# Gated layers of a two-layer transformer: nine of eleven feature pairs as a 2 by 2 block product with seven products

## The chip, the core and the metric

One core of a Trainium2 chip runs the whole program. The metric is the device time of one execution in microseconds (us); lower is better. All times are from the hardware profile or from timed executions.

## What is computed

The reference runs one sequence of 512 tokens with 1024 features, in float32, through a conformer convolution layer, a gated layer, a dilated attention layer, a second gated layer, and then a retention block with its own feed-forward part. The change touches the two gated layers only:

```python
def swiglu(h, w_gate, w_up, w_down):
    return (jax.nn.silu(h @ w_gate) * (h @ w_up)) @ w_down

    h = rmsnorm(x, norm_ffn[i])
    x = x + swiglu(h, ffn_w_gate[i], ffn_w_up[i], ffn_w_down[i])
```

`w_gate` and `w_up` are 1024 x 2816 each, `w_down` is 2816 x 1024. The 2816 hidden features are 22 tiles of 128, or eleven pairs of tiles.

## The kernel before

Features lie on the 128 partitions and the 512 tokens along the free dimension. `xT` is the residual stream (8 tiles of 128 x 512), `R` the reciprocal root of the mean square, broadcast over the partitions.

Every float32 product is made from three reduced-precision products (`mm3`): an operand is split into a rounded high part and the low part that is left, and high x high, high x low and low x high are added in one PSUM bank. For an activation the parts are `xh`, `xl`; for a weight `whi`, `wlo`. Weights come from HBM in blocks of 128 x 1024 elements (`raw`, four buffers). `Stream` loads them in the order of `weight_plan`, and `split_to` makes `whi` on ScalarE (line 127 in the profile's rows is its rounding copy) and `wlo` on VectorE. `get` hands the next block to the matmuls and first splits up to four blocks counted from the one that it hands out; there are four buffers of `whi` and of `wlo`, so the split of a block waits until TensorE has finished with the block four places earlier. Line 80 is the helper `Meter`, through which all VectorE, GpSimd and TensorE instructions are recorded.

Each engine runs its instructions in the order in which the program issues them; that order is written out by hand. `half_tick` is called after every two contraction tiles, and `after(n, fn)` puts a piece of work n ticks later.

A gated layer (`ffn`) takes a pair of feature tiles at a time. `group` multiplies the pair's gate columns with the 8 tiles of the input (2 x 8 x 3 matmuls of 512 tokens), a second `group` the up columns. Then, for each tile, VectorE multiplies both results by `R`, ScalarE applies Silu, VectorE multiplies the two, ScalarE makes the high part `hh` and VectorE the low part `hl` (lines 986 and 990 are the two ScalarE steps). The input's own split for these products is made before the root is known; `R` is applied to the results. `norm_root` gets `R` some 2.5 ticks into the layer. When all 22 tiles are there, four groups over 22 contraction tiles form the down product.

Of the kernel before, what the change touches and what calls it, by code (L numbers as in the profile page):

```python
# [13 lines left out]
S = 512  # L14
# [3 lines left out]
KF = 22  # L18
# [36 lines left out]
POOLW = (0, 0, 0, 0)  # L55
LN1 = (3, 5, 2, 5)
BACK = 2.5
WAIT = 1
ROOT = 0.5
HD_SCALE = 64 ** -0.5  # L60
# [24 lines left out]
class Stream:  # L85


    def __init__(self, nc, V, G, raw_p, w_p, specs, n_raw, n_split):
        self.nc, self.V, self.G = nc, V, G
        self.raw_p, self.w_p, self.specs = raw_p, w_p, specs  # L90
        self.n_raw, self.n_split = n_raw, n_split
        self.raw, self.hl = {}, {}
        self.limit = 1 << 30
        self.on_pool = ()
        self.wait = 0
        self.i_load = self.i_split = self.i_use = 0

    def shape(self, i):
        _, _, nk, cols = self.specs[i]
        return nk, sum(n for _, n in cols)  # L100

    def load_to(self, n):
        while self.i_load < min(n, len(self.specs)):
            w, k0, nk, cols = self.specs[self.i_load]
            nk, nc_ = self.shape(self.i_load)
            t = self.raw_p.tile([128, 1024], F32, tag="raw", name="raw")
            v = t[:, 0:nk * nc_].rearrange("p (k c) -> p k c", k=nk)
            o = 0
            for c0, n_ in cols:
                self.nc.sync.dma_start(  # L110
                    out=v[:, :, o:o + n_],
                    in_=w[k0 * 128:(k0 + nk) * 128, c0:c0 + n_].rearrange("(k p) c -> p k c", p=128),
                )
                o += n_
            self.raw[self.i_load] = t
            self.i_load += 1

    def split_to(self, n):
        while self.i_split < min(n, len(self.specs), self.limit):
            i = self.i_split  # L120
            nk, nc_ = self.shape(i)
            self.load_to(i + 1)
            raw = self.raw.pop(i)[:, 0:nk * nc_]
            h = self.w_p.tile([128, 1024], F32R, tag="whi", name="whi")
            l = self.w_p.tile([128, 1024], F32R, tag="wlo", name="wlo")
            hv, lv = h[:, 0:nk * nc_], l[:, 0:nk * nc_]
            self.nc.scalar.activation(out=hv, in_=raw, func=AF.Copy)  # L127
            E = self.G if i in self.on_pool else self.V
            E.tensor_tensor(out=lv, in0=raw, in1=hv.bitcast(F32), op=ALU.subtract)
            self.hl[i] = (  # L130
                hv.rearrange("p (k c) -> p k c", k=nk),
                lv.rearrange("p (k c) -> p k c", k=nk),
            )
            self.i_split += 1
            self.load_to(self.i_split + self.n_raw - self.wait)

    def get(self):
        i = self.i_use
# [5 lines left out]
def weight_plan(A):  # L144
    specs = []

    def cols(w, c0, n, kt, step=4):
        for k in range(0, kt, step):
            specs.append((w, k, min(step, kt - k), [(c0, n)]))

    for j in range(KD):
        for k, n in ((0, 4), (4, 4)) if j else ((0, 2), (2, 2), (4, 4)):
            specs.append((A["conv_w_pw1"][0], k, n, [(128 * j, 128), (D + 128 * j, 128)]))
    def pair(w, ca, cb, ks=((0, 4), (4, 4))):
        for k, n in ks:
            for c in (ca, cb):
                specs.append((w, k, n, [(c, 256)]))

    pair(A["conv_w_pw2"][0], 0, 256)
    for j in (2, 3):  # L160
        cols(A["conv_w_pw2"][0], 256 * j, 256, KD)

    def ffn(l):
        for j in range(KF // 2):
            cols(A["ffn_w_gate"][l], 256 * j, 256, KD)
            cols(A["ffn_w_up"][l], 256 * j, 256, KD)
        for j in range(4):
# [121 lines left out]
def body(nc, tc, A, out):  # L289
# [3 lines left out]
    with ctx:  # L293
# [284 lines left out]
        with tc.tile_pool(name="c1", bufs=1) as c1, tc.tile_pool(name="c1s", bufs=1, side="right") as c1s:  # L578
# [90 lines left out]
            def add(j, t):  # L669
                V.tensor_tensor(out=cc[j], in0=cc[j], in1=t, op=ALU.add)  # L670
# [302 lines left out]

        def ffn(l, gname, goff):
            with tc.tile_pool(name=f"ff{l}", bufs=1) as fp:
                hh = [fp.tile([128, S], F32R, name=f"hh{k}") for k in range(KF)]
                hl = [fp.tile([128, S], F32R, name=f"hl{k}") for k in range(KF)]
                after(2, norm_root)
                for jj in range(KF // 2):
                    pg = group(KD, *xop)  # L980
                    pu = group(KD, *xop)
                    for m in range(2):
                        j = 2 * jj + m
                        a = tmp.tile([128, S], F32, tag="t1", name="a")
                        V.tensor_tensor(out=a, in0=pg[m], in1=R, op=ALU.mult)
                        ACT.activation(out=a, in_=a, func=AF.Silu)  # L986
                        b = tmp.tile([128, S], F32, tag="t2", name="b")
                        V.tensor_tensor(out=b, in0=pu[m], in1=R, op=ALU.mult)
                        V.tensor_tensor(out=b, in0=a, in1=b, op=ALU.mult)
                        ACT.activation(out=hh[j], in_=b, func=AF.Copy)  # L990
                        V.tensor_tensor(out=hl[j], in0=b, in1=hh[j].bitcast(F32), op=ALU.subtract)
                for j in range(0, KD, 2):
                    resid(group(KF, lambda k: hh[k], lambda k: hl[k]), j, gname, goff)

        ffn(0, "norm_mix", 8)

# [671 lines left out]
```

## Time and profile before

| | |
|---|---|
| median of 3 timed runs | 1663.43 us (1660.7 to 1664.26) |
| the profiled execution | 1660.89 us, its span 1659.1 us |
| granted TensorE clock, mean | 0.995 |
| TensorE busy | 98% of the span, 7972 matmuls |
| VectorE busy | 52%, 1254 instructions |
| ScalarE busy | 35%, 871 instructions |

The span runs from the first to the last instruction. Matmuls are pipelined, so the length that a row gives for one matmul is longer than the distance to the next; the rate is read from starts. For VectorE and ScalarE too the next instruction may begin a little before the recorded end of the last.

### The profile page before, as it was taken

What the parts mean: (1) busy time and instruction counts of PE and PEld (TensorE: products, weight loads), DVE (VectorE), ACT (ScalarE), POOL (GpSimd) and SP (SyncE); (2) the same over time, 40 slices, a digit from 0 to 9 for tenths busy, and PEclk for the clock granted to TensorE, in tenths of its full rate; (3) what the DMA queues carried; (4) which work ended last, traced back from release to release, by engine and by line L of the source; (5) the groups of instructions that cost most, each with busy time, mean ns of one, the idle gap of its engine ahead of it and who ended that gap; (6) DMA issues with size and microseconds to landing.
All of it is one profiled execution on the core that took longest, in us unless ns stands there. A gap on an engine that the chain in (4) does not pass through costs nothing.

```text
span 1659.1 us, 19926 instructions
## 1 busy us (share of the span) xinstructions
PE 1629.4 (98%) x7972; PEld 1366.3 (82%) x7972; DVE 869.2 (52%) x1254; ACT 586.0 (35%) x871; POOL 181.3 (11%) x151
## 2 busy tenths in 40 slices
PE   9998999999999999999999999999999999999997
PEld 6787888888888878888888888888888888888886
DVE  7996644444423345664444434346776545544226
ACT  5623532332322234343323223234543543333210
POOL 4786100000000000000000000000323200000000
PEclk9999999999999999999999999999999999999999
DMA  7331323232232432132323332342232323233321
GB/s 205 116 123 45 102 90 102 89 100 89 85 108 91 128 102 74 52 115 89 98 89 94 102 96 92 105 130 73 64 102 64 127 65 114 89 102 102 102 89 51
DMA packets 157221, 159.85 MB, mean 96 GB/s; under 512 B 6490, under 2 KB 148937, under 8 KB 157129
## 3 DMA queue, kind: packets, MB, share of 16 engines
q1 hardware_dynamic: 157128, 158.59, 30.9%
q8 instruction: 62, 1.02, 0.2%
q14 instruction: 31, 0.25, 0.0%
HBM read 154.56 MB, written 5.57 MB: 97 GB/s over the span
## 4 chain that ended last, share of the span: by engine, by line
PE 85%; DVE 8%; ACT 3%; issue 2%; DMA 1%; POOL 1%; SPq 0%; DVEq 0%; ACTq 0%; POOLq 0%
PE mm L80 73%; PE dn L80 6%; PE pv L80 2%; DMA raw<-in_conv_w_pw 1%; DVE cb L80 1%; DVE cc L80 1%; DVE ca L80 1%; DVE wlo L80 1%; PE o L80 1%; ACT whi L127 1%; DVE y L80 1%; PE po L80 1%; DVE rp L80 0%; DVE sdl L80 0%; PE tl L80 0%
## 5 line engine op out<-in xcount | busy, mean ns | idle before, releaser
L80 DVE TENSOR_TENSOR wlo<-raw,whi 128x1024 fp32r<-128x1024 f32 (+1 forms) x278 | 336.0, 1222 | 519.2 <-ACT whi L127 519.1
L80 PE MATMUL mm<-xh,whi 128*128 128x512 f32 (+1 forms) x1472 | 570.6, 388 | 1.9 <-ACT whi L127 1.5
L80 PE MATMUL mm<-xl,whi 128*128 128x512 f32 (+1 forms) x1472 | 568.2, 386 | 1.6 <-DVE xl L80 1.2
L80 PE MATMUL mm<-xh,wlo 128*128 128x512 f32 (+1 forms) x1472 | 567.8, 386 | 0.4 <-DVE wlo L80 0.4
L127 ACT ACTIVATE whi<-raw 128x1024 fp32r<-128x1024 f32 (+1 forms) x282 | 285.9, 1031 | 522.2 <-PE mm L80 316.8
L80 PEld LDWEIGHTS mm<-xl,whi 128*128 128x128 f32 x1472 | 277.4, 188 | 58.2 <-DVE xl L80 4.1
L80 PEld LDWEIGHTS mm<-xh,whi 128*128 128x128 f32 x1472 | 277.5, 189 | 58.1 <-issue 1.8
L80 PEld LDWEIGHTS mm<-xh,wlo 128*128 128x128 f32 x1472 | 277.3, 188 | 56.7 <-DVE wlo L80 1.4
L80 PE MATMUL mm<-hh,whi 128*128 128x512 f32 x352 | 136.9, 389 | 0.0
L80 PE MATMUL mm<-hl,whi 128*128 128x512 f32 x352 | 136.9, 389 | 0.0
L80 PE MATMUL mm<-hh,wlo 128*128 128x512 f32 x352 | 136.9, 389 | 0.0
L80 POOL TENSOR_TENSOR r<-v,mhalf 128x4 f32<-128x4 f32 x9 | 12.9, 1429 | 986.1 <-DVE v L80 986.1
L80 PEld LDWEIGHTS mm<-hl,whi 128*128 128x128 f32 x352 | 66.1, 188 | 13.8
L80 PEld LDWEIGHTS mm<-hh,wlo 128*128 128x128 f32 x352 | 66.1, 188 | 13.8
L80 PEld LDWEIGHTS mm<-hh,whi 128*128 128x128 f32 x352 | 66.1, 188 | 13.6
L80 PE MATMUL dn<-wlo,gh 128*128 128x512 f32 x176 | 68.6, 390 | 0.1
L80 PE MATMUL dn<-whi,gh 128*128 128x512 f32 x176 | 68.5, 389 | 0.0
L80 PE MATMUL dn<-whi,gl 128*128 128x512 f32 x176 | 68.5, 389 | 0.0
L990 ACT ACTIVATE hh<-b 128x512 fp32r<-128x512 f32 x44 | 27.8, 632 | 78.9 <-DVE b L80 78.9
L80 DVE TENSOR_TENSOR b<-mm,R 128x512 f32<-128x512 f32 x44 | 30.2, 686 | 44.5 <-PE mm L80 44.5
L986 ACT ACTIVATE a<-a 128x512 f32<-128x512 f32 x44 | 27.8, 632 | 72.7 <-DVE a L80 72.7
L80 DVE TENSOR_TENSOR hl<-b,hh 128x512 fp32r<-128x512 f32 x44 | 30.5, 692 | 30.8 <-ACT hh L990 30.8
(257 smaller groups left out, 1780.3 us busy)
## 6 DMA issues: line engine op xcount, KB each, us to landing
raw<-in_ffn_w_gate SPq DMA_DIRECT2D x44, 512.0 KB
raw<-in_ffn_w_up SPq DMA_DIRECT2D x44, 512.0 KB
raw<-in_w_up SPq DMA_DIRECT2D x44, 512.0 KB
raw<-in_ffn_w_down SPq DMA_DIRECT2D x40, 512.0 KB
raw<-in_w_down SPq DMA_DIRECT2D x22, 512.0 KB
raw<-in_w_in SPq DMA_DIRECT2D x20, 512.0 KB
raw<-in_attn_w_qkv SPq DMA_DIRECT2D x18, 512.0 KB
raw<-in_conv_w_pw SPq DMA_DIRECT2D x30, 256.0 KB
```

The costliest lines, as they stand in the source:

```text
L80: return fn(*args, **kw)
L127: self.nc.scalar.activation(out=hv, in_=raw, func=AF.Copy)
L986: ACT.activation(out=a, in_=a, func=AF.Silu)
L990: ACT.activation(out=hh[j], in_=b, func=AF.Copy)
```

## The change

In each gated layer the first two pairs (`NPL = 2`) stay as they were. In the other nine, the pair's gate and up columns together are treated as a 2 by 2 block matrix (two feature tiles by two halves of the contraction), and the input as a 2 by 2 block matrix (two halves of the contraction by two halves of the tokens). The block product is made with seven block products in place of eight. A block of weights is 4 contraction tiles x 128 gate and 128 up columns. One of the seven ("role" 0 to 6) is 24 matmuls of 256 columns into one bank: gate in its first half, up in its second.

On the weight side four loaded blocks (`a11`, `a21`, `a22`, `a12`) give seven operands, with four additions on VectorE (`source`), each of which is then split. `a12` gets a buffer of its own, and loads are issued when the buffer's last use has been split (`free`). On the input side, the blocks are normalized once `R` is known (`normed`), four differences and sums are formed, and seven operands split (`hi`, `lo`); these 26 steps are dealt out three at a time over the first two pairs. An unused tile of 192 bytes a partition (`PADB`) stands ahead of these operands' tiles and moves them. After the products, VectorE combines the seven outputs into four blocks; Silu and the multiply work on 256 tokens and are issued one and two roles later. The high and low parts of hidden features are no longer made in each pair but during the last pair and during the down product, up to three tiles ahead of use (`LOOK`). The program also reserves 128 in place of 1024 bytes for descriptors of GpSimd transfers.

```diff
+NPL = 2
+LOOK = 3
+PADB = 192
...
+        self.loads, self.need = [], []
+        free = {"raw": [], "a12": []}
+        for i, (w, k0, nk, cols) in enumerate(specs):
+            if not isinstance(w, tuple):
+                new = [((i,), [(w, k0, nk, cols)], "raw", i)]
+            elif k0 == 0:
+                new = [((i, n), [(m, k, 4, [(cols + c, 128)]) for m in w], tag, i + e) for n, k, c, tag, e in (
+                    ("a11", 0, 0, "raw", 2), ("a21", 0, 128, "raw", 4), ("a22", 4, 128, "raw", 6), ("a12", 4, 0, "a12", 5))]
+            else:
+                new = []
+            for name, parts, tag, e in new:
+                self.loads.append((name, parts, tag, free[tag], len(free[tag])))
+                free[tag].append(e)
+            n = len(self.loads)
+            self.need.append(n - (3, 1, 1)[k0] if isinstance(w, tuple) and k0 < 3 else n)
...
+    def free(self):
+        if self.i_load == len(self.loads):
+            return False
+        _, _, tag, ends, n = self.loads[self.i_load]
+        n -= self.n_raw - self.wait if tag == "raw" else 1
+        return n < 0 or ends[n] < self.i_split
+    def source(self, i):
+        w, role, _, _ = self.specs[i]
+        if not isinstance(w, tuple):
+            return self.raw.pop((i,))
+        r = {n: self.raw[i - role, n] for n in ("a11", "a21", "a22", "a12") if (i - role, n) in self.raw}
+        add = lambda out, a, b: self.V.tensor_tensor(out=out, in0=a, in1=b, op=ALU.add)
+        if role == 1:
+            self.s = self.sum_p.tile([128, 1024], F32, tag="s1", name="s1", bufs=1)
+            add(self.s, r["a21"], r["a22"])
+        elif role == 2:
+            add(self.s, r["a11"], self.s)
+            add(r["a21"], r["a11"], r["a21"])
+        elif role == 5:
+            add(self.s, r["a12"], self.s)
+        return (r["a11"], self.s, self.s, r.get("a12"), r["a21"], self.s, r["a22"])[role] if role else r["a11"]
 
     def split_to(self, n):
         while self.i_split < min(n, len(self.specs), self.limit):
             i = self.i_split
-            nk, nc_ = self.shape(i)
-            self.load_to(i + 1)
-            raw = self.raw.pop(i)[:, 0:nk * nc_]
+            w, _, nk, _ = self.specs[i]
+            self.load_to(self.need[i])
+            raw = self.source(i)
+            n_ = raw.shape[1]
             h = self.w_p.tile([128, 1024], F32R, tag="whi", name="whi")
             l = self.w_p.tile([128, 1024], F32R, tag="wlo", name="wlo")
-            hv, lv = h[:, 0:nk * nc_], l[:, 0:nk * nc_]
+            hv, lv = h[:, 0:n_], l[:, 0:n_]
             self.nc.scalar.activation(out=hv, in_=raw, func=AF.Copy)
             E = self.G if i in self.on_pool else self.V
             E.tensor_tensor(out=lv, in0=raw, in1=hv.bitcast(F32), op=ALU.subtract)
...
             self.i_split += 1
-            self.load_to(self.i_split + self.n_raw - self.wait)
+            while self.free():
+                self.load_to(self.i_load + 1)
...
-        for j in range(KF // 2):
+        for j in range(NPL):
             cols(A["ffn_w_gate"][l], 256 * j, 256, KD)
             cols(A["ffn_w_up"][l], 256 * j, 256, KD)
+        for j in range(NPL, KF // 2):
+            for role in range(7):
+                specs.append(((A["ffn_w_gate"][l], A["ffn_w_up"][l]), role, 4, 256 * j))
...
-                hh = [fp.tile([128, S], F32R, name=f"hh{k}") for k in range(KF)]
-                hl = [fp.tile([128, S], F32R, name=f"hl{k}") for k in range(KF)]
+                st.sum_p = fp
...
+                blk = [four("xn") for _ in range(4)]
+                tn = [four("tn") for _ in range(4)]
+                if PADB:
+                    fp.tile([128, PADB // 4], F32, name="gap")
+                ops_ = {}
+                def normed(k):
+                    def fn():
+                        for t in range(2):
+                            V.scalar_tensor_tensor(out=blk[2 * (k // 4) + t][:, k % 4], in0=xT[:, k, HALF[t]], scalar=col(pname, poff + k), in1=R[:, HALF[t]], op0=ALU.mult, op1=ALU.mult)
+                    return fn
+                def hi(r, src, sign=1.0):
+                    def fn():
+                        ops_[r] = [four("op", F32R, "op") for _ in range(2)]
+                        ACT.activation(out=ops_[r][0], in_=src, func=AF.Copy, scale=sign)
+                    return fn
+                def lo(r, src, sign=1.0):
+                    return lambda: V.scalar_tensor_tensor(out=ops_[r][1], in0=src, scalar=sign, in1=ops_[r][0].bitcast(F32), op0=ALU.mult, op1=ALU.subtract)
+                def comb(n, a, b, op):
+                    return lambda: V.tensor_tensor(out=tn[n], in0=a, in1=b, op=op)
+                pname, poff = "norm_ffn", 8 * l
+                steps = [normed(k) for k in range(4)] + [
+                    hi(0, blk[0], -1.0), comb(0, blk[0], blk[1], ALU.subtract), hi(1, tn[0]), lo(0, blk[0], -1.0),
+                ] + [normed(k) for k in range(4, 8)] + [
+                    lo(1, tn[0]), comb(1, blk[3], tn[0], ALU.add), hi(2, tn[1]), hi(3, blk[2]),
+                    comb(2, blk[1], blk[3], ALU.subtract), lo(2, tn[1]), hi(4, tn[2]), lo(3, blk[2]),
+                    comb(3, blk[2], tn[1], ALU.subtract), hi(5, blk[3]), lo(4, tn[2]), hi(6, tn[3]), lo(5, blk[3]), lo(6, tn[3]),
+                ]
...
+                def convert(k):
+                    if k % 2 == 0:
+                        hh.append(two(four("hh", F32R, "op")))
+                        hl.append(two(four("hl", F32R, "h" if k else "op")))
+                    x, h, l = (v[k // 2][:, k % 2] for v in (hid, hh, hl))
+                    ACT.activation(out=h, in_=x, func=AF.Copy)
+                    V.tensor_tensor(out=l, in0=x, in1=h.bitcast(F32), op=ALU.subtract)
...
+                def hid_h(k):
+                    converted(k + LOOK + 1)
+                    return hh[k // 2][:, k % 2]
                 after(2, norm_root)
-                for jj in range(KF // 2):
+                for n in range(10):
+                    after(3 + 0.5 * n, lambda: run_steps(3))
+                for jj in range(NPL):
                     pg = group(KD, *xop)
                     pu = group(KD, *xop)
+                    hid.append(two(four("hid")))
                     for m in range(2):
-                        j = 2 * jj + m
                         a = tmp.tile([128, S], F32, tag="t1", name="a")
                         V.tensor_tensor(out=a, in0=pg[m], in1=R, op=ALU.mult)
                         ACT.activation(out=a, in_=a, func=AF.Silu)
                         b = tmp.tile([128, S], F32, tag="t2", name="b")
                         V.tensor_tensor(out=b, in0=pu[m], in1=R, op=ALU.mult)
-                        V.tensor_tensor(out=b, in0=a, in1=b, op=ALU.mult)
-                        ACT.activation(out=hh[j], in_=b, func=AF.Copy)
-                        V.tensor_tensor(out=hl[j], in0=b, in1=hh[j].bitcast(F32), op=ALU.subtract)
+                        V.tensor_tensor(out=hid[jj][:, m], in0=a, in1=b, op=ALU.mult)
+                run_steps(100)
+                GT, UP = HALF
+                todo = []
+                def silu_mul(c, f, t):
+                    g = c[:, GT]
+                    h_ = hid[-1]
+                    def mul():
+                        V.tensor_tensor(out=h_[:, f, HALF[t]], in0=g, in1=c[:, UP], op=ALU.mult)
+                    def act():
+                        ACT.activation(out=g, in_=g, func=AF.Silu)
+                        todo.append(mul)
+                    todo.append(act)
+                def comb2(out, a, b, op):
+                    V.tensor_tensor(out=out, in0=a, in1=b, op=op)
+                    return out
+                for jj in range(NPL, KF // 2):
+                    p = []
+                    hid.append(two(four("hid")))
+                    for role in range(7):
+                        (wh, wl), _, _ = st.get()
+                        now, todo[:] = list(todo), []
+                        for fn in now:
+                            fn()
+                        o = bank("p")
+                        p.append(o)
+                        xh_, xl_ = ops_[role]
+                        for s_ in range(2):
+                            for kk in range(4):
+                                mm3(o[:, HALF[s_]], wh[:, s_, kk], wl[:, s_, kk], xh_[:, kk], xl_[:, kk], kk == 0, kk == 3)
+                        if role == 0:
+                            c1 = scratch("t1")
+                            ACT.copy(c1, o)
+                        elif role == 2:
+                            c2 = comb2(scratch("t2"), o, c1, ALU.add)
+                        elif role == 3:
+                            silu_mul(comb2(c1, o, c1, ALU.subtract), 0, 0)
+                        elif role == 4:
+                            c3 = comb2(scratch("t1"), o, c2, ALU.add)
+                            silu_mul(comb2(scratch("sq"), c3, p[1], ALU.subtract), 1, 1)
+                            comb2(c2, p[1], c2, ALU.subtract)
+                        elif role == 5:
+                            silu_mul(comb2(c2, o, c2, ALU.add), 0, 1)
+                        elif role == 6:
+                            silu_mul(comb2(c3, o, c3, ALU.add), 1, 0)
+                        half_tick()
+                        if jj == KF // 2 - 1 and role in (2, 4):
+                            converted(2 * role - 2)
...
                 for j in range(0, KD, 2):
-                    resid(group(KF, lambda k: hh[k], lambda k: hl[k]), j, gname, goff)
+                    resid(group(KF, hid_h, lambda k: hl[k // 2][:, k % 2]), j, gname, goff)
```

## Rows read from the trace of the kernel before

**Rows 1.** The page's busy times and shares, and granted clock in tenths, 40 slices.

```profile
PE 1629.4 (98%) x7972; PEld 1366.3 (82%) x7972; DVE 869.2 (52%) x1254; ACT 586.0 (35%) x871; POOL 181.3 (11%) x151
PEclk9999999999999999999999999999999999999999
```

**Rows 2.** The chain that ended last, in order of time: start, length, what.

```profile
222.58 350.92 PE mm L80 x1548
```

**Rows 3.** One pair's stretch: length, then busy time and instructions of each engine.

```profile
401.50:423.30 21.80, 21.80 (x98) 18.04 (x97) 10.12 (x14) 6.55 (x8) 0.00 (x0) 1.00 0.32 97
```

**Rows 4.** VectorE's timeline over a pair: start, length, instruction, idle time before.

```profile
400.37 1.23 DVE L80 TENSOR_TENSOR wlo<-raw,whi 128x1024 fp32r<-128x1024 f32 x1 [4.21 <-ACT whi L127]
401.51 0.68 DVE L80 TENSOR_TENSOR a<-mm,R 128x512 f32<-128x512 f32 x1
404.21 0.69 DVE L80 TENSOR_TENSOR b<-mm,R 128x512 f32<-128x512 f32 x1 [2.02 <-PE mm L80]
405.01 0.69 DVE L80 TENSOR_TENSOR b<-a,b 128x512 f32<-128x512 f32 x1
406.40 0.69 DVE L80 TENSOR_TENSOR hl<-b,hh 128x512 fp32r<-128x512 f32 x1 [0.70 <-ACT hh L990]
407.01 0.68 DVE L80 TENSOR_TENSOR a<-mm,R 128x512 f32<-128x512 f32 x1
407.61 0.68 DVE L80 TENSOR_TENSOR b<-mm,R 128x512 f32<-128x512 f32 x1
408.45 0.69 DVE L80 TENSOR_TENSOR b<-a,b 128x512 f32<-128x512 f32 x1 [0.16 <-ACT a L986]
...
423.27 0.68 DVE L80 TENSOR_TENSOR a<-mm,R 128x512 f32<-128x512 f32 x1
```

**Rows 5.** TensorE's timeline: starts of 256-column matmuls in two stages, the down product's first.

```profile
170.79 0.40 PE L80 MATMUL mm<-zs,whi 128*128 128x256 f32 x2
...
184.32 0.40 PE L80 MATMUL mm<-zs,whi 128*128 128x256 f32 x2
...
448.21 0.39 PE L80 MATMUL mm<-hh,whi 128*128 128x512 f32 x1
...
1253.28 0.28 PE L80 MATMUL mm<-mxh,whi 128*128 128x256 f32 x1
...
1259.75 0.28 PE L80 MATMUL mm<-mxh,whi 128*128 128x256 f32 x1
```

**Rows 6.** ScalarE's timeline: R of the first layer, and the pair of rows 4.

```profile
222.62 0.59 ACT L494 COPY R<-pr 128x512 f32<-128x512 f32 x1 [3.63 <-PE pr L80]
...
405.74 0.63 ACT L990 ACTIVATE hh<-b 128x512 fp32r<-128x512 f32 x1 [2.82 <-DVE b L80]
...
409.18 0.63 ACT L990 ACTIVATE hh<-b 128x512 fp32r<-128x512 f32 x1 [0.76 <-DVE b L80]
409.72 1.99 ACT L127 ACTIVATE whi<-raw 128x1024 fp32r<-128x1024 f32 x2
...
415.59 1.06 ACT L127 ACTIVATE whi<-raw 128x1024 fp32r<-128x1024 f32 x1 [3.89 <-issue]
```

**Rows 7.** VectorE's and ScalarE's timelines elsewhere: scaled forms of 512, operations of 256.

```profile
55.77 0.75 DVE L80 SCALAR_TENSOR_TENSOR ca<-up,cv,ca 128x512 f32<-128x512 f32 x1
56.42 0.75 DVE L80 SCALAR_TENSOR_TENSOR cb<-up,cv,cb 128x512 f32<-128x512 f32 x1
...
1278.08 0.42 ACT L1504 ACTIVATE xh<-xT 128x256 fp32r<-128x256 f32 x1
1278.41 0.59 ACT L1503 ACTIVATE xT<-xT,cv 128x256 f32<-128x256 f32 x1
...
1282.22 3.23 DVE L80 TENSOR_TENSOR xT<-xT,lnq 128x256 f32<-128x256 f32 x8
```

**Rows 8.** Stretches of convolution and gated stage: last two numbers are transfer share, GB/s.

```profile
60.00:100.00 40.00, 38.94 (x190) 32.30 (x189) 38.18 (x51) 21.41 (x30) 33.68 (x22) 1.00 0.46 139
...
222.00:440.00 218.00, 218.00 (x966) 180.59 (x965) 100.73 (x120) 66.06 (x81) 0.00 (x0) 1.00 0.31 96
```

More of the change, by code (lines that the diff above doesn't have):

```diff
@@ L95, in __init__ @@
         self.wait = 0
+        self.sum_p = None
         self.i_load = self.i_split = self.i_use = 0
-    def shape(self, i):
-        _, _, nk, cols = self.specs[i]
-        return nk, sum(n for _, n in cols)
-    def load_to(self, n):
[L103 to L107, printed above, removed]
-            o = 0
[L109 to L115, printed above, removed]
-            self.i_load += 1
+        self.loads, self.need = [], []
@@ new lines, in load_to @@
+    def load_to(self, n):
+        while self.i_load < min(n, len(self.loads)):
+            name, parts, tag, _, _ = self.loads[self.i_load]
+            p, b = (self.raw_p, None) if tag == "raw" else (self.sum_p, 1)
+            t = p.tile([128, 1024], F32, tag=tag, name="raw", bufs=b)
+            o = 0
+            for w, k0, nk, cols in parts:
+                nc_ = sum(n_ for _, n_ in cols)
+                v = t[:, o:o + nk * nc_].rearrange("p (k c) -> p k c", k=nk)
+                o += nk * nc_
+                c = 0
+                for c0, n_ in cols:
+                    self.nc.sync.dma_start(
+                        out=v[:, :, c:c + n_],
+                        in_=w[k0 * 128:(k0 + nk) * 128, c0:c0 + n_].rearrange("(k p) c -> p k c", p=128),
+                    )
+                    c += n_
+            self.raw[name] = t[:, 0:o]
+            self.i_load += 1
@@ L129, in split_to @@
             E.tensor_tensor(out=lv, in0=raw, in1=hv.bitcast(F32), op=ALU.subtract)
[L130 to L133, printed above, removed]
+            if isinstance(w, tuple):
+                self.hl[i] = tuple(v.rearrange("p (s k c) -> p s k c", s=2, k=nk) for v in (hv, lv))
+            else:
+                self.hl[i] = tuple(v.rearrange("p (k c) -> p k c", k=nk) for v in (hv, lv))
             self.i_split += 1
-            self.load_to(self.i_split + self.n_raw - self.wait)
+            while self.free():
+                self.load_to(self.i_load + 1)
     def get(self):
@@ L975, in ffn, with four, two @@
             with tc.tile_pool(name=f"ff{l}", bufs=1) as fp:
-                hh = [fp.tile([128, S], F32R, name=f"hh{k}") for k in range(KF)]
-                hl = [fp.tile([128, S], F32R, name=f"hl{k}") for k in range(KF)]
+                st.sum_p = fp
+                def four(name, dt=F32, tag="h"):
+                    return fp.tile([128, 4, 256], dt, tag=tag, name=name, bufs=11 if tag == "h" else 14)
+                def two(t):
+                    return t.rearrange("p (k a) t -> p k (a t)", k=2)
@@ new lines, in run_steps @@
+                def run_steps(n):
+                    for _ in range(min(n, len(steps))):
+                        steps.pop(0)()
+                hid, hh, hl = [], [], []
+                def convert(k):
[5 more added lines that the diff above has]
+                    V.tensor_tensor(out=l, in0=x, in1=h.bitcast(F32), op=ALU.subtract)
@@ L978, in ffn, with converted @@
+                done_k = [0]
+                def converted(n):
+                    while done_k[0] < min(n, KF):
+                        convert(done_k[0])
+                        done_k[0] += 1
+                def hid_h(k):
+                    converted(k + LOOK + 1)
+                    return hh[k // 2][:, k % 2]
                 after(2, norm_root)
-                for jj in range(KF // 2):
+                for n in range(10):
+                    after(3 + 0.5 * n, lambda: run_steps(3))
@@ new lines, in scratch @@
+                def scratch(tag):
+                    return tmp.tile([128, S], F32, tag=tag, name="c")
+                for jj in range(NPL, KF // 2):
[30 more added lines that the diff above has]
+                            converted(2 * role - 2)
@@ L992, in ffn @@
+                while todo:
+                    now, todo[:] = list(todo), []
+                    for fn in now:
+                        fn()
                 for j in range(0, KD, 2):
-                    resid(group(KF, lambda k: hh[k], lambda k: hl[k]), j, gname, goff)
+                    resid(group(KF, hid_h, lambda k: hl[k // 2][:, k % 2]), j, gname, goff)
         ffn(0, "norm_mix", 8)
@@ L1653 @@
     from concourse.bass_utils import run_bass_kernel_spmd
-    nc = bacc.Bacc("TRN2", target_bir_lowering=False, num_devices=1, dynamic_dma_scratch_size=1024)
+    nc = bacc.Bacc("TRN2", target_bir_lowering=False, num_devices=1, dynamic_dma_scratch_size=128)
     given = {n: np.ascontiguousarray(inputs[n]) for n in _INS}
```

## The prediction

> **What bounds the kernel now.** I read the page's busy shares first, then the chain that ended last, then single pairs of features in the timeline. TensorE is busy 98% of the span at full granted clock (the digits are all 9) [rows 1]. The chain is one run of TensorE over the first gated stage and its down product, 350.9 us with 1548 matmuls [rows 2]. So a gated pair costs what its 96 matmuls cost. VectorE starts the same multiply at 401.51 and at 423.27, 21.76 us apart [rows 4], and in one such stretch TensorE is busy throughout, VectorE 10.12 us, ScalarE 6.55 us [rows 3]. The reader should keep the 10.12: it is what the change adds to.
>
> **TensorE's part.** Seven roles of 24 matmuls of 256 columns, 168, replace 96 of 512. The 512-column form thus starts every 21.76 / 96 = 0.227 us. The 256-column form occurs already in two other stages: 114 starts in 13.53 us are 0.1187, 54 in 6.47 us are 0.1198 [rows 5]. I take 0.1193; a role is then 24 x 0.1193 = 2.86 us and a pair 20.04. The gain is 1.72 us a pair, less than the eighth that the column count says (2.72), since each start carries a fixed part. 18 pairs: 31.0 us, if TensorE still sets the pace.
>
> **VectorE's part.** In a pair it now subtracts seven low parts instead of four, adds four weight sums of 1024, combines seven outputs of 512 and multiplies four halves of 256. What counts is start to start: a subtraction of 1024 at 400.37 lets the next start at 401.51, 1.14 us later (I use 1.135, the mean of such steps), a 512 one 0.60 later (407.01 to 407.61) [rows 4]. For 256 the clean step has no row; eight dependent ones take 3.23 us, 0.40 each, and that is the upper end, 0.33 (0.60 less half of the 0.535 that 512 more elements cost) the lower [rows 7]; I take 0.33, as these multiplies don't depend on each other. An operation that reads the one just before it starts 0.80 after it, not 0.60 (404.21 to 405.01) [rows 4]; the combinations hold one. Sum of the work: 11 x 1.135 + 7 x 0.60 + 0.20 + 4 x 0.33 = 18.2 us, below 20.04.
>
> But order matters. For roles 1, 2 and 5 the weight sum is made on VectorE, rounded on ScalarE, then subtracted on VectorE, with nothing queued between. The same triangle stands in rows 4 and 6: the multiply of 405.01 (0.69 long) ends 405.70, ScalarE starts 405.74, takes 0.63, VectorE resumes 406.40. For 1024 elements: 1.23 + 0.04 + 1.06 + 0.03 = 2.36 us from sum to subtraction [rows 4, 6], against 1.135 without the wait. Role 2 has a second sum to fill it (0.08 is left), roles 1 and 5 nothing: 2 x 1.22. So 18.2 + 2.45 + 0.08 = 20.73 us of VectorE a pair. That is more than TensorE's 20.04, so VectorE becomes the pace setter, and the pair gains 1.03 us instead of 1.72.
>
> **The start of a stage.** In the two pairs that stay as they are, the seven input operands are now made as well. None can start before R (223.2 us, the copy at 222.62 of 0.59) [rows 6]. VectorE then has: 16 scaled halves, 7 low parts, 4 differences. The scaled form steps 0.65 at 512 (55.77 to 56.42) [rows 7], so about 0.39 at 256 and 1.19 at 1024 (estimates by 1.07 ns an element): 6.3 + 8.4 + 4.5 = 19.2 us. Further the two old epilogues without their high and low parts, 4.0 each (407.01 to 408.45 and 0.60 for one half, 2.0) [rows 4], three plain splits 3.4, the sums and splits of roles 1 and 2, 3.49 each, and some 2.8 us of waiting for ScalarE and for weight buffers. Together 40.4, so VectorE reaches role 3 of the first new pair's weights at 263.6. TensorE would be at that pair's start at 448.2 - 9 x 21.76 = 252.4 [rows 5]. Splits run three roles ahead, 3 x 2.86 = 8.6 us, and VectorE is 11.2 us late, so the lead is gone before the first new pair is under way, and VectorE leads from there.
>
> **Sum for a stage.** Weights of role 2 are last to come. In the ninth new pair they are done at 263.6 + 7 x 20.73 + 19.8 = 428.5 (VectorE's order in a pair begins with role 3's split and ends with role 2's, a multiply and a combination, 0.33 + 0.60 after it: 20.73 - 0.93 = 19.8); five roles follow, 14.3 us: 442.8, where the down product began at 448.2. Gain 5.4. In the down product the conversion of hidden features, formerly done in each pair (two 0.6 steps and their waits), now runs just ahead of use, behind the late VectorE. Six of 22 are made before; the seventh comes some 2.0 us late and the eighth 0.4, by the same steps: minus 2.4. Net 3.0 a stage. The second layer runs the same function: 6.0 in all. 1660.9 - 6.0 = 1654.9 for the profiled execution, which lies 2.5 us under the median of the runs: 1657.4, so 1657.
>
> **What is free.** ScalarE: 7 x 1.06 + 0.6 + 4 x 0.42 = 9.6 us of 20.7; cover enough, except for its order (below). The transfers keep their bytes in runs half as long, two issues for one, on SP's queue, which has nothing else here; a stage with runs of 512 bytes already moves 139 GB/s at a share of 0.46, the gated stage 96 at 0.31 [rows 8], the same per byte. The tightest block (a22, issued behind role 4's split, needed at the next role 1) has about 9 us for 512 KB. If that cover were gone, each us late would be a us in VectorE's queue. The 192 bytes move operand addresses. No row has these addresses; the 256-column rows differ by 1%, 0.2 us a pair, hidden under VectorE (0 to 3.6 us in all if it were not).
>
> [...] VectorE's 1024-element operation lasts 1.23 us and hands over after 1.14 [rows 4]. [...]
>
> **The rivals.**
> *TensorE still leads.* If VectorE's waits hide (18.2 us of work against 20.04), the stage ends at 252.4 + 9 x 20.04 = 432.8, 15.4 earlier: 1663.4 - 30.8 = 1633. For it: VectorE's pure work is smaller. Against: the sums' triangle is in program order, and the backlog at the start.
>
> *ScalarE's order makes VectorE wait once more; slower.* At role 0 ScalarE has queued: Silu of the last combination (VectorE's last operation of the pair before), the copy of role 0's output, then the rounding of role 4. By steps of about 0.33 and 0.50 (1278.08 to 1278.41 for 256 [rows 7]; between 409.18 and 409.72 for 512 [rows 6]) the rounding ends 2.0 us into role 0, VectorE wants it at 1.47: 0.58 us a pair, 4.6 a stage. Net minus 1.6 a stage: 1663.4 + 3.3 = 1667. It turns the sign once a pair costs VectorE more than 20.73 + 3.0/8 = 21.1. I keep it out of the forecast because it hangs on half a microsecond between two drifting engines; it is its nearest neighbour. More waits of the kind at 22.0 a pair give 1678.
>
> *Each operation holds VectorE for its whole length.* 11 x 0.09 + 7 x 0.09 + 4 x 0.09 = 2.0 more a pair, 16 a stage: 1689. Rows 4 speak against it.
>
> *It doesn't do what it says:* 256-column matmuls at over 0.1295 us would take the whole gain; rows 5 show none.
>
> **How the numbers follow.** A measurement tells a change from none at about 0.2%, 3.3 us. Forecast, VectorE at 20.3 to 21.0 a pair (1650 to 1661): 0.38. TensorE leads, or nearly (1633 to 1650): 0.17. ScalarE's order or more such waits (1661 to 1680): 0.38, of which a third is within 3.3 us. Whole lengths or slow matmuls: 0.07. Faster: 0.30 of the forecast's 0.38 and the 0.17, 0.47. Same: 0.08 and 0.12, 0.20. Slower: 0.33. The range reaches from near the first rival to the 22.0 of the second: 1636 to 1680; the likeliest case's own is 1650 to 1661.
>
> **What would show it.** Between the first and the last new pair VectorE's repeat should be 20.7 us, its idle before the subtractions of roles 1 and 5 about 1.1 each, with TensorE waiting for a low part once or twice a pair, about 0.7 us in sum; 256-column starts 0.119. The down product should begin about 5 us earlier against R and then wait 2 us for a hidden feature's low part. A repeat near 20.0 with TensorE without gaps proves the first rival, 21.3 with idle before role 4's subtraction the second. The prediction is wrong if VectorE's step in a loaded queue is not that of rows 4.

## The result and the profile after

The changed kernel takes 1675.71 us (median of 4 runs, 1674.97 to 1676.43) against 1663.39 of the kernel before: ratio 1.0077, 95% interval 1.0064 to 1.009. It is slower by 12 us; forecast was 6 us faster. The profiled execution took 1675.11 us, its span is 1673.3, 14.2 longer than before.

First the page's busy times:

```profile
PE 1614.5 (96%) x9268; PEld 1399.8 (84%) x9268; DVE 1081.6 (65%) x1524; ACT 660.4 (39%) x993; POOL 181.5 (11%) x151
PEclk9999999999999999999999999999999999999999
```

TensorE has less to do than in [rows 1], 1614.5 instead of 1629.4 us, and yet the span is longer: it now waits. VectorE has 212 us more. The granted clock is 9 in every digit as before, 0.991 in the mean (0.995 before). VectorE's timeline over one new pair in the middle of the first layer shows why (start, length, instruction, idle time before it):

```profile
287.85 1.23 DVE L84 TENSOR_TENSOR wlo<-raw,whi 128x1024 fp32r<-128x1024 f32 x1 [0.45 <-ACT whi L178]
288.99 0.42 DVE L84 TENSOR_TENSOR hid<-c 128x256 f32<-128x256 f32 x1
289.32 1.22 DVE L84 TENSOR_TENSOR s<-raw,s 128x1024 f32<-128x1024 f32 x1
291.75 1.23 DVE L84 TENSOR_TENSOR wlo<-s,whi 128x1024 fp32r<-128x1024 f32 x1 [1.21 <-ACT whi L178]
292.89 0.68 DVE L84 TENSOR_TENSOR c<-p,c 128x512 f32<-128x512 f32 x1
293.49 1.22 DVE L84 TENSOR_TENSOR wlo<-raw,whi 128x1024 fp32r<-128x1024 f32 x1
...
296.36 0.68 DVE L84 TENSOR_TENSOR c<-p,c 128x512 f32<-128x512 f32 x1
297.08 0.69 DVE L84 TENSOR_TENSOR c<-c,p 128x512 f32<-128x512 f32 x1
297.68 0.68 DVE L84 TENSOR_TENSOR c<-p,c 128x512 f32<-128x512 f32 x1
298.28 1.22 DVE L84 TENSOR_TENSOR s<-raw 128x1024 f32<-128x1024 f32 x1
300.71 1.22 DVE L84 TENSOR_TENSOR wlo<-s,whi 128x1024 fp32r<-128x1024 f32 x1 [1.21 <-ACT whi L178]
...
302.79 1.21 DVE L84 TENSOR_TENSOR s<-raw,s 128x1024 f32<-128x1024 f32 x1
303.92 1.22 DVE L84 TENSOR_TENSOR raw<-raw 128x1024 f32<-128x1024 f32 x1
305.21 1.23 DVE L84 TENSOR_TENSOR wlo<-s,whi 128x1024 fp32r<-128x1024 f32 x1
306.35 0.42 DVE L84 TENSOR_TENSOR hid<-c 128x256 f32<-128x256 f32 x1
...
308.42 0.42 DVE L84 TENSOR_TENSOR hid<-c 128x256 f32<-128x256 f32 x1
309.29 1.23 DVE L84 TENSOR_TENSOR wlo<-raw,whi 128x1024 fp32r<-128x1024 f32 x1 [0.45 <-ACT whi L178]
```

The repeat is 309.29 - 287.85 = 21.44 us, against 21.76 in [rows 4] and the 20.73 forecast. VectorE never waits for TensorE here. It waits three times for ScalarE: 1.21 us between the sum and the low part of role 5 (291.75), the same for role 1 (300.71), and 0.45 in front of role 4's low part (309.29). These are idle times from the recorded end of the operation before; from start to start, as a queue's sum counts, the first two cost 2.43 - 1.14 = 1.29 each (289.32 to 291.75), and the third 0.54 (308.42 to 309.29 is 0.87, where the same step takes 0.33 at 288.99). In between it goes from start to start in 1.14 us for 1024 elements, as in [rows 4].

TensorE's timeline around role 2, and the start and course of the first down product:

```profile
283.79 0.50 PE L84 MATMUL p<-op,whi 128*128 128x256 f32 x2 [0.47 <-ACT whi L178]
285.05 0.38 PE L84 MATMUL p<-op,wlo 128*128 128x256 f32 x1 [0.76 <-DVE wlo L84]
...
288.80 0.40 PE L84 MATMUL p<-op,whi 128*128 128x256 f32 x2
...
290.57 0.40 PE L84 MATMUL p<-op,whi 128*128 128x256 f32 x2
...
449.16 0.39 PE L84 MATMUL mm<-hh,whi 128*128 128x512 f32 x1
...
458.19 0.50 PE L84 MATMUL mm<-hh,whi 128*128 128x512 f32 x1 [0.46 <-ACT hh L1084]
459.53 0.50 PE L84 MATMUL mm<-hl,whi 128*128 128x512 f32 x1 [0.84 <-DVE hl L84]
...
499.79 0.40 PE L84 MATMUL mm<-hh,whi 128*128 128x512 f32 x1
...
502.60 0.40 PE L84 MATMUL mm<-hh,whi 128*128 128x512 f32 x1
```

Once a pair TensorE stands still for role 2's weights, here 0.47 and then 0.76 us (the second inside a role, for the low part). The 256-column form starts every 0.118 us here (15 starts in 1.77), as forecast; in other stretches of the layer it starts every 0.113 us (last section). The 512-column form of the down product does not keep its pace: 12 starts in 2.81 us are 0.234, where it had 0.227. R's copy and the end of the first layer, from ScalarE's timeline and the chain in order of time:

```profile
223.59 0.59 ACT L549 COPY R<-pr 128x512 f32<-128x512 f32 x1 [3.63 <-PE pr L84]
```

```profile
580.62 0.79 PE pc L84 x8
```

From R to the down product: 449.16 - 223.59 = 225.57 us; before, 448.21 - 222.62 = 225.59 [rows 5, 6]. The new pairs gain nothing at all. From there to the next sum of squares: 131.46 us, before 573.50 - 448.21 = 125.29 [rows 2, 5]. The down product loses 6.2 us a layer, 12.3 in two; the other 1.9 us of the longer span lie outside the gated layers, 1.0 of them ahead of the first R, which the profiled executions of the variants below reach at anything from 222.0 to 225.3 us although they do not differ in what comes ahead of it.

### The profile page after: what moved, and what is told of

Read it like the earlier page. It is cut to its first block, busy times and chain, and to the rows that moved or that the text cites. A ratio compares the mean times of both kernels' runs of the same rounds, so it can differ in the third digit from the quotient of the medians.

```text
span 1673.3 us, 23107 instructions
## 1 busy us (share of the span) xinstructions
PE 1614.5 (96%) x9268; PEld 1399.8 (84%) x9268; DVE 1081.6 (65%) x1524; ACT 660.4 (39%) x993; POOL 181.5 (11%) x151
## 4 chain that ended last, share of the span: by engine, by line
PE 64%; DVE 21%; ACT 7%; issue 4%; DMA 1%; POOL 1%; SPq 0%; DVEq 0%; ACTq 0%; POOLq 0%
PE mm L84 47%; DVE wlo L84 7%; PE dn L84 6%; PE p L84 5%; ACT whi L178 5%; DVE c L84 3%; DVE s L84 3%; PE pv L84 2%; DMA raw<-in_conv_w_pw 1%; DVE cb L84 1%; PE o L84 1%; DVE cc L84 1%; DVE ca L84 1%; DVE op L84 1%; DVE y L84 1%
## 5 line engine op out<-in xcount | busy, mean ns | idle before, releaser
L84 PE MATMUL p<-op,whi 128*128 128x256 f32 x2016 | 355.9, 281 | 11.4 <-ACT whi L178 6.3
L84 PE MATMUL mm<-xh,whi 128*128 128x512 f32 (+1 forms) x896 | 347.6, 388 | 2.0 <-ACT whi L178 0.9
L84 PE MATMUL mm<-xl,whi 128*128 128x512 f32 (+1 forms) x896 | 344.4, 384 | 2.2 <-DVE xl L84 1.7
L84 PE MATMUL mm<-xh,wlo 128*128 128x512 f32 (+1 forms) x896 | 343.9, 384 | 0.0
L84 PEld LDWEIGHTS p<-op,whi 128*128 128x128 f32 x2016 | 308.1, 189 | 15.1 <-ACT whi L178 9.5
L84 PE MATMUL p<-op,wlo 128*128 128x256 f32 x1008 | 284.9, 283 | 15.7 <-DVE wlo L84 15.5
L84 PEld LDWEIGHTS p<-op,wlo 128*128 128x128 f32 x1008 | 192.2, 191 | 21.7 <-DVE wlo L84 21.7
L84 PEld LDWEIGHTS mm<-xl,whi 128*128 128x128 f32 x896 | 170.2, 190 | 36.6 <-DVE xl L84 4.5
L84 PEld LDWEIGHTS mm<-xh,whi 128*128 128x128 f32 x896 | 170.2, 190 | 36.2 <-issue 1.9
L84 PEld LDWEIGHTS mm<-xh,wlo 128*128 128x128 f32 x896 | 169.8, 190 | 33.3 <-DVE wlo L84 0.4
L84 PEld LDWEIGHTS mm<-hl,whi 128*128 128x128 f32 x352 | 66.1, 188 | 18.3 <-DVE hl L84 3.3
```

The source lines that it names most:

```text
L84: return fn(*args, **kw)
```

## Experiments

The theory after the result: VectorE's queue, with its three waits for ScalarE, sets the pace of the new pairs; the 192 bytes set only the distance of TensorE's starts, for better with 256 columns, for worse with 512. The rival: TensorE's starts at the new addresses set the pace, and VectorE only follows; then the repeat changes with the gap and not with VectorE's order. Times are medians; the kernel before took 1662.8 to 1663.4 beside them. Where a layer's pairs differ, the repeat is that of its last ones.

| kernel | median us | ratio to before, 95% interval | new pair, first layer, us |
|---|---|---|---|
| changed kernel | 1675.71 | 1.0077 (1.0064 to 1.009) | 21.44 |
| no gap | 1667.23 | 1.0029 (1.0017 to 1.0041) | 21.44 |
| copy later | 1667.10 | 1.0024 (1.0015 to 1.0034) | 20.97 |
| hidden features split earlier | 1675.23 | 1.0074 (1.0059 to 1.0089) | 21.44 |
| useless addition | 1686.65 | 1.0138 (1.0121 to 1.0155) | 22.05 |
| role 5's sum earlier | 1644.27 | 0.9887 (0.9872 to 0.9901) | 19.60 |
| both sums earlier | 1630.48 | 0.9806 (0.9789 to 0.9824) | 19.79 |
| both, no gap | 1639.13 | 0.9857 (0.9842 to 0.9871) | 20.16 |
| both, useless addition | 1637.94 | 0.9838 (0.9809 to 0.9868) | 19.79 |
| both, gap 64 | 1636.09 | 0.9832 (0.9813 to 0.9851) | 19.79 |
| both, gap 128 | 1638.41 | 0.9854 (0.984 to 0.9869) | 19.94 |

**No gap.**

```diff
-PADB = 192
+PADB = 0
```

> The changed kernel without the 192 byte gap. Theory (VectorE sets the pace of the new pairs at 21.44 us; the gap moves addresses and these set only the distance of matmul starts): the pair's repeat stays at 21.44 though the 256-column starts go back from 0.1177 to about 0.120; the 512-column starts of the down products, 0.234 with the gap, go back to 0.2267, which is 528 x 0.0075 = 4.0 us a layer: 1675.7 - 8 = about 1668. Rival 1 (the slow down products come from the tiles' shape, four blocks of 256, not from the address): no change, 1676. Rival 2 (TensorE's starts matter in the new pairs): the pairs get slower by 168 x 0.0023 = 0.4 us each and the 8 us are given back, 1675.

VectorE's timeline, the same addition in three successive pairs, and TensorE's in the down product:

```profile
302.92 1.22 DVE L84 TENSOR_TENSOR raw<-raw 128x1024 f32<-128x1024 f32 x1
324.36 1.22 DVE L84 TENSOR_TENSOR raw<-raw 128x1024 f32<-128x1024 f32 x1
345.80 1.22 DVE L84 TENSOR_TENSOR raw<-raw 128x1024 f32<-128x1024 f32 x1
```

```profile
519.96 0.39 PE L84 MATMUL mm<-hh,whi 128*128 128x512 f32 x1
...
521.32 0.39 PE L84 MATMUL mm<-hh,whi 128*128 128x512 f32 x1
```

The repeat is 21.44 still, though the 256-column starts went to 0.120: TensorE's rate does not matter in the pairs, and the rival falls. The 512-column starts are back at 1.36 / 6 = 0.227, and 8.5 us are back in the time. Both as the theory has it.

**Copy later.** ScalarE's copy of role 0's output is issued one role later, behind the rounding of role 4's weights.

```diff
-                            ACT.copy(c1, o)
+                            todo.append(lambda c1=c1, o=o: ACT.copy(c1, o))
```

> The changed kernel with one ScalarE step moved: the copy of role 0's output is issued after the rounding of role 4's weights instead of before it. Theory (the prediction's second rival: ScalarE's order makes VectorE wait 0.45 us for that rounding in every pair): the wait in front of role 4's low part goes, the repeat falls from 21.44 to about 21.0, 8 x 0.45 = 3.6 us a layer, 1675.7 - 7 = about 1668.5. Rival (the wait comes from the Silu or the weight buffer, and moves): no change.

The time fell by 8.6 us to 1667.10, the repeat by 0.47; the wait in front of role 4's low part is gone. The wait that the prediction had left out of its sum is real, and this is its price.

**Hidden features split earlier.** `LOOK = 6` instead of 3.

> Hidden features are split six tiles ahead of their use instead of three; all else as in the changed kernel. Theory (some 2 us a layer of waits at the start of the down product are the lateness of these splits in VectorE's queue behind weight blocks): TensorE's idle time in front of hidden features' parts falls from about 2 us a layer to under 1, the total by 2 to 3 us to 1673. Rival (VectorE is late whatever the order, since its backlog stems from the pairs): no change, 1676.

No change (1675.23): the rival holds. VectorE is late at the start of the down product because of its backlog, and another order of the same late work does not help. With both sums earlier (below) these waits are gone without it.

**A useless addition**, `comb2(scratch("sq"), c1, c1, ALU.add)` at role 2, in the changed kernel and in the one with both sums earlier:

> The changed kernel with one useless VectorE addition of 512 in each new pair, at role 2, whose result nobody reads. Theory (VectorE sets the pace): each pair is 0.6 us longer, 18 x 0.6 = 10.8, about 1686. Rival (VectorE has slack): no change.

> The same useless addition in the kernel with both sums earlier. Theory (there TensorE sets the pace, VectorE has 19.0 of 19.8 us in the first layer and of 19.1 in the second): the first layer takes nearly all of it for nothing, the second, with no slack, up to 0.5 a pair: 0 to 5 us over that run's 1630. Rival (VectorE sets the pace there too): 10.8 us more, 1641.

In the changed kernel it costs 10.9 us and 0.6 us in every repeat: VectorE sets the pace. In the other kernel the repeat of the first layer stays at 19.79, so there VectorE has slack. The total is 7.5 us above that kernel's median all the same, more than the 0 to 5 expected, with single runs from 1629 to 1641. Between the two profiled executions the difference sits in TensorE's own starts; the second layer's new pairs in the chain, first without the addition, then with it:

```profile
808.39 1.24 DVE wlo L84
...
809.67 127.90 PE p L84 x1126
```

```profile
774.33 169.64 PE p L84 x1438
```

127.90 / 1126 = 0.1136 us against 169.64 / 1438 = 0.1180, both without a wait inside. Ahead of 809.67 TensorE had waited for VectorE, and its starts before that wait have 0.1134. From R to the down product this layer takes 204.5 us without the addition and 210.3 with it, 5.8 of the 6.3 us between the two profiled spans. That the addition causes this is not shown: both distances occur within single executions of one kernel (last section), and one run with the addition, 1629.09, is as fast as those without it.

**Role 5's sum earlier.** The sum for role 5 is issued between role 4's rounding and role 4's low part, so that VectorE adds while ScalarE rounds.

```diff
             self.nc.scalar.activation(out=hv, in_=raw, func=AF.Copy)
+            if isinstance(w, tuple) and w and self.specs[i][1] == 4:
+                self.V.tensor_tensor(out=self.s, in0=self.raw[i - 4, "a12"], in1=self.s, op=ALU.add)
...
-        elif role == 5:
-            add(self.s, r["a12"], self.s)
```

> Of the two earlier sums only role 5's (issued ahead of role 4's low part); role 1's stays. Theory (each hidden wait is worth its own 1.21 us as long as VectorE sets the pace): repeat 21.44 - 1.21 = 20.2, still above TensorE's 19.8 (19.1 in the second layer); 8 x 1.21 = 9.7 us a layer, 1675.7 - 19 = about 1656. Rival (the two waits hide one another, or the gain of both came from the loads that are asked for earlier): under a quarter of the 45 us that both gave, above 1665.

VectorE's timeline in that kernel, from role 4 to role 5 and role 1's sum:

```profile
306.22 1.22 DVE L84 TENSOR_TENSOR s<-raw,s 128x1024 f32<-128x1024 f32 x1
307.36 1.22 DVE L84 TENSOR_TENSOR wlo<-raw,whi 128x1024 fp32r<-128x1024 f32 x1
308.49 0.42 DVE L84 TENSOR_TENSOR hid<-c 128x256 f32<-128x256 f32 x1
308.83 1.22 DVE L84 TENSOR_TENSOR wlo<-s,whi 128x1024 fp32r<-128x1024 f32 x1
...
315.35 1.21 DVE L84 TENSOR_TENSOR s<-raw 128x1024 f32<-128x1024 f32 x1
317.77 1.23 DVE L84 TENSOR_TENSOR wlo<-s,whi 128x1024 fp32r<-128x1024 f32 x1 [1.21 <-ACT whi L176]
```

The repeat falls by 1.84 us, from 21.44 to 19.60, not by the 1.21 expected. From start to start role 5's wait is worth 1.29, and the addition, which now starts 1.14 us ahead of role 4's low part, fills that wait (0.54) too: 1.83. Role 5's low part follows without idle time. No load is asked for earlier here, so the expectation's rival falls. Role 1's 1.21 is still there. VectorE at 19.60 is a little faster than TensorE's 168 starts of 0.118, 19.8, so it catches up on the late start: from 303.95 us on TensorE runs through the layer without a gap. (Up to there its starts were the denser 0.1134, 19.05 a pair, and it waited for VectorE.) Hence 1644.27 instead of the expected 1656, already 1.1% below the kernel before.

**Both sums earlier.** Role 1's sum goes ahead of role 0's low part as well; the blocks it reads must then be loaded one role sooner.

```diff
-            self.need.append(n - (3, 1, 1)[k0] if isinstance(w, tuple) and k0 < 3 else n)
+            self.need.append(n - (1, 1, 1)[k0] if isinstance(w, tuple) and k0 < 3 else n)
...
             self.nc.scalar.activation(out=hv, in_=raw, func=AF.Copy)
+            self.early(i)
...
+    def early(self, i):
+        w, role, _, _ = self.specs[i]
+        if not isinstance(w, tuple) or role not in (0, 4):
+            return
...
+        if role == 0:
+            self.s = self.sum_p.tile([128, 1024], F32, tag="s1", name="s1", bufs=1)
+            add(self.s, r("a21"), r("a22"))
+        else:
+            add(self.s, r("a12"), self.s)
...
-        if role == 1:
-            self.s = self.sum_p.tile([128, 1024], F32, tag="s1", name="s1", bufs=1)
-            add(self.s, r["a21"], r["a22"])
...
-        elif role == 5:
-            add(self.s, r["a12"], self.s)
```

> The weight sums of roles 1 and 5 are issued one role earlier, ahead of the low part of role 0 and of role 4, so that ScalarE rounds the sum while VectorE makes that low part. Same instructions, gap kept at 192. Theory (VectorE sets the pace, and its two waits of 1.21 us for the rounding of a sum are what puts it above TensorE): VectorE's pair falls from 21.44 to about 19.0, TensorE's 168 x 0.1177 = 19.8 takes over, about 1.6 us a pair from the first or second new pair on: 14 us a layer, and the late hidden features (2 us a layer) go too: 1675.7 - 28 to - 32 = 1644 to 1648, below the kernel before. Rival (ScalarE's order or TensorE's weight loads set the pace, the waits on VectorE only reflect it): repeat stays above 21, time within 4 us of 1676.

VectorE's timeline around roles 0, 1 and the next role 4, and the chain in order of time:

```profile
288.89 1.23 DVE L84 TENSOR_TENSOR s<-raw 128x1024 f32<-128x1024 f32 x1 [0.30 <-DMA raw<-in_ffn_w_up]
290.04 1.22 DVE L84 TENSOR_TENSOR wlo<-raw,whi 128x1024 fp32r<-128x1024 f32 x1
...
301.13 1.22 DVE L84 TENSOR_TENSOR s<-raw,s 128x1024 f32<-128x1024 f32 x1
302.27 1.22 DVE L84 TENSOR_TENSOR wlo<-raw,whi 128x1024 fp32r<-128x1024 f32 x1
```

```profile
263.73 169.12 PE p L84 x1438
432.84 37.22 PE mm L84 x159
```

TensorE runs from role 3 of the first new pair to the end of the layer, 60 roles of 24 starts, and on into the down product without waiting once: 169.12 / 1438 = 0.1176 us a start in the mean. The three waits for ScalarE are gone; waits for the transfer of the sum's block have come (0.30 us in these rows). VectorE's slack covers them in this layer; in the second the longest is 1.62 us (at 799.70), and TensorE stands still once for 0.55 (the wait ahead of 809.67 above). The time is 1630.48 us, 45 below the changed kernel and 1.9% below the kernel before. Expected were 28 to 32. The profiled span is 42.5 shorter, and the first layer, from R to the down product, 16.0 (the 15.4 of the prediction's first rival); the second gives 21.1, by the starts of 0.113 us there; and each down product 2.2, for the hidden features now come in time. The expectation had 14 a layer and 2 for the hidden features; what it lacked is mostly the second layer's denser starts.

**Both, no gap**, and **both, gaps of 64 and 128 bytes.**

> The earlier sums and no gap. Theory: in the new pairs TensorE now sets the pace, so its starts count: 168 x 0.120 = 20.2 in place of 19.8, plus 0.4 x 9 = 3.5 us a layer; the down products gain 4.0 a layer. Both nearly cancel: within 2 us of the run with the earlier sums and the gap, about 1646. Rival (the gap does not touch the down products): 7 us slower than that run.

> Both sums earlier, gap 64 bytes instead of 192. TensorE sets the pace there, so the time reads the distance of matmul starts. Theory (a gap of any size takes the operands off a common boundary): 256-column starts below 0.1198 and 512-column starts at 0.234 as with 192, about 1630. Rival 1 (the distance depends on the gap's size): another pair of distances, anything from 1622 (fast in both) to 1640. Rival 2 (only gaps of 192 work): as without a gap, 1639.

> The same with 128 bytes. Theory (any gap): about 1630, starts as with 192. Rival 1 (the distance depends on the size): distances between those of 64 and 192, 1622 to 1640. Rival 2 (only 192): 1639.

The first layer's new pairs in the chain, for no gap, 64 and 128:

```profile
265.38 172.81 PE p L84 x1438
```

```profile
264.07 169.64 PE p L84 x1438
```

```profile
264.78 170.91 PE p L84 x1438
```

| gap, bytes | 256 columns, start to start, us | 512 columns (hidden features), us | median, us |
|---|---|---|---|
| 0 | 0.1202 | 0.227 | 1639.13 |
| 64 | 0.1180 | 0.231 | 1636.09 |
| 128 | 0.1189 | 0.229 | 1638.41 |
| 192 | 0.1176, a mean of 0.1135 and 0.1178; 0.1180 with the useless addition | 0.234 | 1630.48; 1637.94 |

The distance of the starts depends on the gap's size (the first rival of the last two expectations; their theory, any gap does the same, misses), and a denser 256-column form goes with a slower 512-column one. The expectation for no gap, within 2 us of the run with both sums earlier, misses too: it is 8.7 slower, near the rival's 7, though not for the rival's reason, since the gap does change the down products (0.227 against 0.234). Against the kernel with the useless addition, whose starts are 0.1180 in both layers, the gap of 192 gives back in the pairs (0.0022 x 3000 = 6.6 us) what it takes from the down products (2 x 528 x 0.0075 = 7.9): 1639.13 against 1637.94, nearly nothing. The 8.7 us by which the kernel without the addition beats no gap would then come mostly from stretches of denser starts; this is argued from its one profiled execution, not shown for the other runs. So the order of the sums, not the gap, makes this version the best.

## Why the prediction was wrong, point by point

*What held.* VectorE becomes the pace setter, from the first new pair on: its role 3 was split at 265.33 where the prediction's 263.6 counts from an R 1.0 us earlier. TensorE's 256-column starts are 0.118 or 0.113 (0.1193 taken); at 0.1134 one costs half of the 0.227 of 512 columns, so the fixed part that the prediction gives each start is not seen there. TensorE stands still once a pair, at role 2, for 1.1 to 1.2 us in two parts (0.7 expected), and where its starts are the denser ones for 0.34 more at role 1. The two sums of roles 1 and 5 cost VectorE 1.29 each from start to start (1.22 reckoned). Transfers (a share of 0.34 from 287.85 to 309.29) and ScalarE's busy time are hidden; the latter is 8.9 us a pair (9.6 in the prediction, whose terms add up to 9.7). VectorE's timeline refutes the rival of whole lengths: operations of 1.22 us follow each other by 1.14.

*The step that failed is the sum of VectorE's pair, 20.73 us; it measured 21.44.* The prediction worked out a wait for ScalarE in front of role 4's low part, priced it at 0.58 and kept it out "because it hangs on half a microsecond between two drifting engines". It is there in the middle of the layer, 0.54 us from start to start, and delaying the copy behind role 4's rounding takes 0.47 out of the repeat. The rest of the 0.71 is small: each of the three pairs of sum and subtraction (2.43 from start to start at 289.32 and 298.28, where 2.36 was reckoned) has ScalarE begin some 0.07 later after the addition, 0.21 in all; the combination that reads the one before it starts 0.72 after it and not 0.80 (296.36 to 297.08), which takes 0.08 off; about 0.04 lies in the other steps. Over eight repeats 8 x 0.71 = 5.7 us a layer, and that eats the 5.4 forecast: the down product starts as long after R as before (225.57 against 225.59). The second rival, with its own point of turning at 21.1, is what happened in the pairs; its 1667 lacks the slower 512-column starts.

*The second term that was mis-sized is the down product.* Forecast were 2.4 us of late hidden features a layer, and about that is seen (0.46 and 0.84 us at 458.19 and 459.53 are the first of them; with both sums earlier 2.2 us go). But 6.2 are lost: 528 starts x 0.0075 = 4.0 more come from the 512-column starts at 0.234. The prediction bounded the gap's effect by the 256-column rows only, at 0 to 3.6 us in all, and did not ask which other stage reads tiles in the displaced place (`hh`, which takes over the operands' tiles). The experiment without the gap gives 8.5 us back, with the pairs unchanged.

*The sum.* Forecast for the two layers: -6.0. Measured: 2 x (0.0 + 6.2) = +12.3, and 1.9 outside. Of the difference of 18.3, 10.8 are VectorE's pair (2 x 5.4, all of the gain) and 7.9 the 512-column starts; the hidden features, 0.2 a layer less late than forecast, take 0.4 off.

*The first rival* is what the change gives with the sums earlier: forecast 1633, measured 1630.48. The mechanism is the rival's, TensorE leading, but that the number fits so well is partly luck: against the kernel before, the two layers' pairs gain 16.0 and 21.1 us where it had 15.4 each, and each down product loses 4.0 that it did not have.

## What to carry to other kernels

Where two in-order engines hand a tile to and fro, make the queue's list with its waits, not its busy time: three waits of 0.5 to 1.2 us, not VectorE's 18.5 us of work, decided this change, and a wait whose price can be worked out belongs in the sum. Put independent work between the hand-over and the answer: moving two additions by one step turned 0.8% slower into 1.9% faster. A change of addresses is to be followed to every stage that reads the tile; here it counted only where TensorE set the pace: 4.0 us in each down product, nothing in the changed kernel's new pairs, whose repeat was 21.44 us with and without the gap.

## What the runs showed of the hardware

The distance of TensorE's starts changes with the gap ahead of the operands, in opposite directions for the two widths: 0.1202 us without it and 0.1134 to 0.1189 with it for 256 columns, 0.227 and 0.229 to 0.234 for 512 (table above).

With the gap of 192 bytes there is more to it, which I had not expected: the 256-column starts have two distances, 0.1134 and 0.1178 us, both at a granted clock of 1.00, and they change from one to the other only at a break, a step between two starts of 0.19 us or more in the changed kernel's trace, mostly a wait. The changed kernel shows both in successive pairs of a layer. From 288.80 to 290.57 it is 0.118 (above); after the wait for role 2 of the next pair it is 3.40 / 30 = 0.1133:

```profile
307.41 0.39 PE L84 MATMUL p<-op,whi 128*128 128x256 f32 x2
...
310.81 0.39 PE L84 MATMUL p<-op,whi 128*128 128x256 f32 x2
```

With both sums earlier the first layer has 0.1135 up to a step of 0.22 us between two starts at 280.17 and 0.1178 after it; the second has 0.113 throughout. With 64 bytes the second layer's starts have 0.1133 from 772.77 to 807.79 (309 starts) and 132.89 / 1126 = 0.1180 after a wait of 0.72 us for this low part, in the chain:

```profile
807.62 1.24 DVE wlo L84
808.90 132.89 PE p L84 x1126
```

Without the gap, 0.120, and with 128 bytes, 0.119, every stretch of the new pairs has the one distance, in the changed order of sums and, for no gap, in the old one with its waits in every pair. So a denser layer does not set one of these kernels apart from another. Over the new pairs' 3024 starts the two distances lie 3024 x 0.0044 = 13 us apart (an estimate). Where TensorE sets the pace and both distances were seen, or the gap is the same, the single runs scatter accordingly: 1628 to 1634 (192 bytes), 1629 to 1641 (with the useless addition), 1632 to 1637 (64 bytes), against 1639 to 1640 without the gap and 1637 to 1639 with 128. That this scatter comes from the two distances is argued, since only one execution of each has a trace. Which of the two a stretch gets, and why there are two, no run here settles.
